# Attention of layer 0 on one core: values weighted by unscaled exponentials, bias and maximum in one VectorE operation, modulation vectors on VectorE

## The chip, the cores and the metric

One Trainium2 chip, of which the program uses one core: TensorE (PE; its loads of the stationary operand are shown as PEld), VectorE (DVE), ScalarE (ACT), GpSimd (POOL) and SyncE (SP), which issues nearly all DMAs here. The metric is the time of one execution on the device, in microseconds; lower is better. Everything is computed in float32, for the large products as sums of three products of halves ("hi" and "lo") of the operands.

## The reference

The whole reference is a block with two layers (layer 0 with a pool mixer and neighbourhood attention, layer 1 with a scan over time) and a second block behind it. The change touches layer 0's attention and the vectors that modulate its later stages. Cut to that:

```python
def context_attention(q, k, v):                       # 256 context tokens, 8 heads of 64
    s = jnp.einsum('bqhd,bkhd->bhqk', q, k) * (NA_HEAD_DIM ** -0.5)
    p = jax.nn.softmax(s, axis=-1)
    return jnp.einsum('bhqk,bkhd->bqhd', p, v).reshape(B, L, D_NA)

def neighbourhood_attention(q, k, v, k_ctx, v_ctx, rpb):   # 512 tokens, a grid of 8 rows by 64
    def row_block(args):
        ...
        s_lat = jnp.where(col_ok[:, None, :], s_lat + bias, NEG_INF)
        s = jnp.concatenate([s_lat.reshape(...), s_ctx], axis=-1)
        p = jax.nn.softmax(s, axis=-1)
        ...
        return (jnp.einsum('bhqrk,brkhd->bqhd', p_lat, v_band)
                + jnp.einsum('bhqc,bchd->bqhd', p_ctx, v_ctx))

mod = silu_c @ ada_w[i] + ada_b[i]                    # six modulation vectors of 1024, twice (x and ctx)
sh1, sc1, gt1, sh2, sc2, gt2 = jnp.split(mod, N_MOD, axis=-1)
```

## The kernel before, in words

The order of instructions on each engine is set by a scheduler that plays the program through with its own estimate of times; the code only gives the data dependences, the buffers and, with `issue_after`, some positions. Each engine then works through its list in order, and a waiting instruction holds up all behind it.

`even_mixer` is the first half of layer 0. After the products for keys, values and queries it calls `attend` six times: twice for the 256 context tokens (`qt` 0 and 1, 128 queries each, 256 keys per head) and four times for the 512 grid tokens (`b` 0 to 3, 128 queries each, 256 keys of a window and the 256 of the context). In each call the heads go in pairs (`hb` 0 to 3). For one head:

- the scores `S` (PSUM tile `a`, 128 queries by 256 or 512 keys) are one or two products on TensorE (lines 1202, 1208, 1210);
- VectorE adds the bias `nab` to the window's half (line 1211) and takes the negated maximum of each row (1212, or 1203 for the context);
- ScalarE takes the exponential with that maximum as bias and the row's sum as a by-product (1214);
- VectorE takes the reciprocal of the sum (1215) and multiplies the exponentials by it (1216);
- `pv` turns the 128 by 128 pieces of the result on TensorE (1241, into PSUM tile `b`), copies them out as `pT` (1243, any engine) and multiplies them with the values. There the values are the stationary operand (128 by 64) and `pT` is the moving one (128 columns), and the two heads of a pair write to two halves of the partitions of the PSUM tile `O` (1247). `O` comes out with channels on partitions, as the next stage wants it.

Behind each pair, `next(self.fill)` places a piece of the pool mixer's products (18 products, lines 590 to 592) and now and then its VectorE and ScalarE work (`pool_group`, lines 1161 to 1179). `pump` places one step of `ada_vec`: a group of 256 columns of the modulation weights is loaded in four pieces (`adaw`, two buffers) and multiplied with the two input vectors in 16 steps (`ada_step`), either by ScalarE and GpSimd together (lines 729, 732 and 733: scale on one, add on the other) or, where `on_dve` is true, by VectorE alone (725 and 727). Twelve such groups belong to this stage: six run before `attend` on VectorE, and from line 1142 on, where `on_dve` is set to false, six on ScalarE and GpSimd. `ada_sum` turns the sums on TensorE (745) and adds them up (747, 751).

When the six calls are over, the last piece of the pool mixer has to be finished (VectorE's chain of lines 1169 to 1176, TensorE's line 1178) before the next stage's products (`evout`, lines 590 to 592 again) find their inputs; these are split into halves by lines 596 and 597, and their weights by 583 and 584.

Of the kernel before, what the change touches and what calls it, by code (L numbers as in the profile page):

```python
# [10 lines left out]
F32 = mybir.dt.float32  # L11
# [3 lines left out]
AF = mybir.ActivationFunctionType  # L15
ALU = mybir.AluOpType
AX = mybir.AxisListType
# [532 lines left out]
class Prog:  # L550
# [496 lines left out]
    def even_mixer(self, act, ap, kv, h):  # L1047

        tc, nc = self.tc, self.nc
# [7 lines left out]
        def cols(ps, w, m, g):  # L1057
            _, v, n, o = g
            for k in range(8):
                s = slice(k * 256 + m * 128, k * 256 + (m + 1) * 128)  # L1060
                bi = self.mm3(ps[:, :n], (w[0][:, s], w[1][:, s]), h(k, g), k == 0, k == 7)
            return bi
# [3 lines left out]
        for u, g in self.pair_order(4, self.halves(groups)):  # L1066
            _, v, n, o = g
# [12 lines left out]
        with ExitStack() as ctx:  # L1080
            E = ctx.enter_context
            p1 = E(tc.tile_pool(name="ev1", bufs=2))
            p2 = E(tc.tile_pool(name="ev2", bufs=2))
# [6 lines left out]
            for u in (6, 7):  # L1090
                w = self.wsplit(self.i["evin"][u])
                c0 = (u - 6) * 256
                for tt in range(6):
                    ps = self.pt("mm")
                    for k in range(8):
                        s = slice(k * 256, (k + 1) * 256)
                        hk = h(k, ("x" if tt < 4 else "c", 0, 128, tt * 128))
                        bi = self.mm3(ps[:, :256], hk, (w[0][:, s], w[1][:, s]), k == 0, k == 7)
                    if tt % 3 == 2:
                        self.pump(bi)  # L1100
                    if tt < 4:
                        vs = p1.tile([128, 256], F32, name="vs", tag="psum_w")
# [5 lines left out]
            for u in (2, 3):  # L1108
                w = self.wsplit(self.i["evin"][u])
                for m in range(2):  # L1110
                    mb = u * 2 + m - 4
                    for g in groups:
                        n = g[2]
                        ps = self.pt("mm")
                        bi = cols(ps, w, m, g)
# [9 lines left out]
            def pooling():  # L1125
                for u in (0, 1):
                    w = self.wsplit(self.i["evin"][u])
                    for m in range(2):
                        pss = [self.pt("mm") for g in groups]
                        for k in range(8):  # L1130
                            s = slice(k * 256 + m * 128, k * 256 + (m + 1) * 128)
                            for ps, g in zip(pss, groups):
                                self.mm3(ps[:, :g[2]], (w[0][:, s], w[1][:, s]), h(k, g), k == 0, k == 7)
                            yield
                        for ps, g in zip(pss, groups):
                            self.pool_group(p1, u * 2 + m, ps, g[2], g[3], poolw, po)
# [2 lines left out]
            self.adatag = "st"  # L1139

            self.fill = pooling()
            self.on_dve = False
            for qt in range(2):
                self.attend(p2, qt, None, qP, kT, vd, vctx, *ahl)
            for b in range(4):
# [33 lines left out]
        nc.scalar.activation(po[:, gi, o:o + n], ps[:, :n], AF.Copy, scale=self.col("psc", gi))  # L1179

    def attend(self, p2, qt, b, qP, kT, vd, vctx, chi, clo):
        nc = self.nc
        O = self.pt("st")
        if b is not None:
            ws = WSTART[b]
            vwin = p2.tile([128, 2, 512], F32, name="vwin", tag="vwin")
            for r in range(8):
                nc.sync.dma_start(vwin[(r % 4) * 32:(r % 4) * 32 + 32, r // 4, :], vd[r * 64 + ws:r * 64 + ws + 32, :])
        for hb in range(4):
            if b is not None:  # L1190
                nab = p2.tile([128, 2, 256], F32, name="nab", tag="nab")
                nc.sync.dma_start(nab, self.i["nab"][b][:, hb * 512:(hb + 1) * 512].rearrange("p (h k) -> p h k", h=2))
            es = []
            for hh in range(2):
                r = slice(hh * 64, hh * 64 + 64)
                S = self.pt("a")
                e = p2.tile([128, 512], F32, name="e", tag="e", bufs=3)
                m = p2.tile([128, 4], F32, name="m", tag="m", bufs=4)
                if b is None:
                    n = 256  # L1200
                    q = qP[r, hb, NX + qt * 128:NX + (qt + 1) * 128]
                    nc.tensor.matmul(S[:, :256], q, kT[r, hb, NX:], start=True, stop=True)
                    nc.vector.tensor_reduce(m[:, 0:1], S[:, :256], AX.X, ALU.max, negate=True)
                    vs = [vctx[:, 0], vctx[:, 1]]
                else:
                    n = 512
                    q = qP[r, hb, b * 128:(b + 1) * 128]
                    nc.tensor.matmul(S[:, :256], q, kT[r, hb, :NX].rearrange("p (r c) -> p r c", c=64)[:, :, ws:ws + 32],
                                     start=True, stop=True)
                    nc.tensor.matmul(S[:, 256:], q, kT[r, hb, NX:], start=True, stop=True)  # L1210
                    nc.vector.tensor_tensor(S[:, :256], S[:, :256], nab[:, hh, :], ALU.add)
                    nc.vector.tensor_reduce(m[:, 0:1], S, AX.X, ALU.max, negate=True)
                    vs = [vwin[:, 0], vwin[:, 1], vctx[:, 0], vctx[:, 1]]
                nc.scalar.activation(e[:, :n], S[:, :n], AF.Exp, bias=m[:, 0:1], accum_out=m[:, 1:2])
                nc.vector.reciprocal(m[:, 2:3], m[:, 1:2])
                nc.vector.tensor_scalar(e[:, :n], e[:, :n], m[:, 2:3], None, ALU.mult)
                es.append(e[:, :n])
            bi = self.pv(p2, O[:, hb * 128:(hb + 1) * 128], es, [[v[:, h * 64:(h + 1) * 64] for v in vs] for h in (hb * 2, hb * 2 + 1)])
            for _ in range(1 if b is None else 1 + hb % 2):
                with self.tc.issue_after(bi.ins):  # L1220
                    next(self.fill, None)
            if hb == 3 and (b is not None or qt == 0):
                self.pump(bi)
        if b is None:
            o = NX + qt * 128
            dst = lambda t: t[:, :, o:o + 128]
            src = O.rearrange("p (k t) -> p k t", k=4)
        else:
            dst = lambda t: t[:, :, :NX].rearrange("p k (r b c) -> p k r b c", r=8, b=4)[:, :, :, b, :]
            src = O.rearrange("p (k r c) -> p k r c", k=4, r=8)  # L1230
        self.split_sb(dst(chi), dst(clo), src)
# [677 lines left out]
    def causal(self, t2, i, kind, mask, Q, K, vm, QD, KD, vdt, chi, clo):  # L1909
        nc = self.nc  # L1910
        n = (i + 1) * 128
        qs = slice(i * 128, (i + 1) * 128)
        O = self.pt("st")
        v = vm if kind == 0 else vdt
        for hb in range(4):
            es = []
            for h in (hb * 2, hb * 2 + 1):
# [13 lines left out]
                es.append(s[:, :n])  # L1931
            self.pv(t2, O[:, hb * 128:(hb + 1) * 128], es, [[v[:, k, h * 64:(h + 1) * 64] for k in range(i + 1)] for h in (hb * 2, hb * 2 + 1)])
        kb = slice(kind * 4, kind * 4 + 4)
        self.split_sb(chi[:, kb, qs], clo[:, kb, qs], O.rearrange("p (k t) -> p k t", k=4))

# [17 lines left out]
```

## Time and profile before

| | before |
|---|---|
| median of 3 runs | 3166.5 us (3166.19 to 3166.78) |
| profiled execution, its own time | 3169.68 us |
| span of its profile | 3167.8 us |
| granted TensorE clock, mean over the span | 0.923 |
| PE busy | 2825.9 us (89%) |
| PEld busy | 2343.8 us (74%) |
| DVE busy | 1786.6 us (56%) |
| ACT busy | 1552.0 us (49%) |
| POOL busy | 1138.5 us (36%) |

Busy time is an average over very different stages. The stage of the change lies between about 174 us (the first scores) and 345 us (the next stage's products run), some 5% of the span. Records of TensorE are pipelined and their ends are modelled, so in its rows the distance from one start to the next counts, not the length of a record. A float32 product shows as two records (two passes), a turn as one.

### The profile page before, as it was taken

How to read it: one execution, taken by the hardware profiler on the slowest of the kernel's cores; microseconds unless marked ns; L12 is line 12 of the kernel's file. 1: busy time of each engine (PE TensorE's matmuls, PEld its weight loads, DVE VectorE, ACT ScalarE, POOL GpSimd, SP SyncE). 2: the span in 40 equal slices, each digit the busy share in tenths (PEclk: the TensorE clock that was granted, in tenths of full speed). 3: DMA queues.
4: the chain of work that ended last, by engine and by line, in shares of the span. 5: the costliest groups of instructions: out<-in, count | busy, mean ns of one | idle time of the engine just before them, and what ended most of it. 6: DMA issues, size and time to landing. Idle time of an engine off the chain costs nothing.

```text
span 3167.8 us, 50960 instructions
## 1 busy us (share of the span) xinstructions
PE 2825.9 (89%) x19290; PEld 2343.8 (74%) x19290; DVE 1786.6 (56%) x3557; ACT 1552.0 (49%) x3104; POOL 1138.5 (36%) x1500
## 2 busy tenths in 40 slices
PE   6999889999996899886777769699997999989999
PEld 6967778888885688764666658577876885678887
DVE  8466383444448725758688732644456654556364
ACT  3246556666664633554566532455543444544341
POOL 4013436667675212045666640245543110010000
PEclk9989989999998899987688879799998996999999
DMA  5323213333331565432223231244541220022222
GB/s 224 127 82 98 104 50 128 117 126 127 113 114 61 190 194 156 162 123 84 73 96 103 79 113 53 99 171 170 179 150 56 80 87 7 14 80 90 103 96 85
DMA packets 137589, 345.69 MB, mean 109 GB/s; under 512 B 16385, under 2 KB 48769, under 8 KB 120065
## 3 DMA queue, kind: packets, MB, share of 16 engines
q1 hardware_dynamic: 137344, 342.43, 31.6%
q8 instruction: 153, 2.51, 0.3%
q14 instruction: 92, 0.75, 0.1%
HBM read 293.35 MB, written 49.02 MB: 108 GB/s over the span
## 4 chain that ended last, share of the span: by engine, by line
PE 34%; DVE 8%; ACT 6%; POOL 5%; DMA 4%; issue 2%; SPq 0%; ACTq 0%; POOLq 0%; DVEq 0%
PE mm L590 7%; PE mm L591 7%; PE mm L592 7%; POOL acc L733 2%; DMA adaw<-in_ada_dram 2%; PE a L1288 2%; ACT wh L583 1%; PE st L1247 1%; PE a L329 1%; POOL M L428 1%; POOL Mt L427 1%; PE y L520 1%; DVE G L387 1%; PE a L1920 1%; PE a L1923 1%
## 5 line engine op out<-in xcount | busy, mean ns | idle before, releaser
L733 POOL TENSOR_TENSOR acc<-acc,adat 128x256 f32<-128x256 f32 x658 | 574.9, 896 | 539.2 <-ACT acc L729 434.0
L584 DVE TENSOR_TENSOR wl<-wr,wh 128x2048 fp32r<-128x2048 f32 (+3 forms) x145 | 317.6, 2190 | 361.1 <-ACT wh L583 358.7
L732 ACT ACTIVATE adat<-adaw,silu 128x256 f32<-128x256 f32 x644 | 319.4, 508 | 262.9 <-POOL acc L733 164.0
L583 ACT CAST wh<-wr 128x2048 fp32r<-128x2048 f32 (+2 forms) x147 | 266.8, 1815 | 232.1 <-PE mm L591 218.7
L590 PE MATMUL mm<-fh,wh 128*128 128x512 f32 (+1 forms) x1008 | 350.2, 356 | 14.0 <-DVE relu L1015 9.8
L591 PE MATMUL mm<-fl,wh 128*128 128x512 f32 (+1 forms) x1008 | 353.1, 352 | 2.2 <-DVE fl L597 2.2
L592 PE MATMUL mm<-fh,wl 128*128 128x512 f32 (+1 forms) x1008 | 352.0, 351 | 0.9 <-DVE wl L584 0.9
L590 PE MATMUL mm<-h_xhi,wh 128*128 128x512 f32 (+1 forms) x784 | 277.7, 359 | 3.6 <-ACT h_xhi L596 2.5
L591 PE MATMUL mm<-h_xlo,wh 128*128 128x512 f32 (+1 forms) x784 | 278.2, 357 | 1.8 <-DVE h_xlo L686 1.5
L592 PE MATMUL mm<-h_xhi,wl 128*128 128x512 f32 (+1 forms) x784 | 278.1, 357 | 0.0
L664 POOL TENSOR_TENSOR acc<-acc,t 128x256 f32<-128x256 f32 x127 | 109.1, 867 | 345.0 <-ACT t L662 342.2
L590 PEld LDWEIGHTS mm<-fh,wh 128*128 128x128 f32 x1008 | 192.1, 191 | 42.1 <-DVE relu L1015 12.1
L591 PEld LDWEIGHTS mm<-fl,wh 128*128 128x128 f32 x1008 | 191.7, 190 | 27.6 <-DVE fl L597 4.0
L592 PEld LDWEIGHTS mm<-fh,wl 128*128 128x128 f32 x1008 | 192.0, 191 | 26.2 <-DVE wl L584 1.1
L1039 DVE TENSOR_TENSOR y<-mm,y 128x512 f32<-128x512 f32 (+1 forms) x184 | 99.5, 559 | 152.1 <-PE mm L592 151.6
L590 PE MATMUL mm<-h_hi,wh 128*128 128x512 f32 (+1 forms) x408 | 160.7, 398 | 6.3 <-ACT h_hi L685 6.3
L592 PEld LDWEIGHTS mm<-h_xhi,wl 128*128 128x128 f32 x784 | 149.0, 190 | 21.4 <-issue 0.2
L590 PEld LDWEIGHTS mm<-h_xhi,wh 128*128 128x128 f32 x784 | 147.6, 190 | 23.3 <-ACT h_xhi L596 2.8
L591 PEld LDWEIGHTS mm<-h_xlo,wh 128*128 128x128 f32 x784 | 148.9, 191 | 20.8 <-DVE h_xlo L686 1.7
L427 POOL TENSOR_TENSOR Mt<-M 128x30 f32<-128x30 f32 (+14 forms) x240 | 141.7, 591 | 58.1 <-PE f L443 23.6
L591 PE MATMUL mm<-h_lo,wh 128*128 128x512 f32 (+1 forms) x408 | 160.3, 394 | 0.0
L592 PE MATMUL mm<-h_hi,wl 128*128 128x512 f32 (+1 forms) x408 | 159.6, 393 | 0.0
(451 smaller groups left out, 6929.6 us busy)
## 6 DMA issues: line engine op xcount, KB each, us to landing
adaw<-in_ada_dram SPq DMA_DIRECT2D x256, 256.0 KB, 2.7
wr<-in_w_dram SPq DMA_DIRECT2D x64, 1024.0 KB, 4.8
wr<-in_wup_dram SPq DMA_DIRECT2D x22, 1024.0 KB, 4.7
base<-b SPq DMA_DIRECT2D x32, 384.0 KB, 3.1
ZU<-vt SPq DMA_DIRECT2D x192, 64.0 KB, 2.5
wr<-in_wdn_dram SPq DMA_DIRECT2D x16, 704.0 KB, 4.1
wr<-in_win_dram SPq DMA_DIRECT2D x9, 1024.0 KB, 4.7
wr<-in_evin_dram SPq DMA_DIRECT2D x8, 1024.0 KB, 4.8
```

The costliest lines, as they stand in the source:

```text
L329: nc.tensor.matmul(ps[:, c], bk[g][:, c0 + c].rearrange("p a t -> p (a t)"), G[:, :na, c0 + c, :], start=True, stop=True)
L427: nc.gpsimd.tensor_tensor(t, a, b, ALU.mult)
L583: nc.scalar.copy(hi[:, :n], raw[:, :n])
L584: (eng or nc.vector).tensor_tensor(lo[:, :n], raw[:, :n], hi[:, :n], ALU.subtract)
L590: mm(out, lhs[0], rhs[0], start=first, stop=False)
L591: mm(out, lhs[0], rhs[1], start=False, stop=False)
L592: return mm(out, lhs[1], rhs[0], start=False, stop=last)
L664: nc.gpsimd.tensor_tensor(acc, acc, sq, ALU.add)
L732: nc.scalar.activation(t, w, AF.Copy, scale=s)
L733: nc.gpsimd.tensor_tensor(acc, acc, t, ALU.add)
L1039: nc.vector.tensor_tensor(yb, ps[:, :n], yb, ALU.add)
L1288: bi = nc.tensor.matmul(ps[:, :256], wcol(m, k), z[:, k, o], start=k == 0, stop=k == early - 1)
```

## The change

`attend` is rewritten from the scores on:

- for the grid tokens one VectorE operation adds the bias to all 512 scores, negates the sum, writes it to `e` in SBUF and takes the row's minimum; the bias tile `nab` is 512 wide now, its second half filled with zeros by GpSimd. The exponential reads `e` in SBUF with scale -1 in place of `S` in PSUM;
- the exponentials are not scaled. They are turned and copied out (the first head of a pair by VectorE, the second by ScalarE), and in the product with the values `pT` is the stationary operand (128 by 128) and the values are the moving one (64 columns). `O` now has queries on partitions;
- once per call, the reciprocals of eight sums are taken and `O` (128 by 512) is multiplied by them into `o`, and four turns on TensorE bring `o` to the layout that `O` had;
- the line `on_dve = False` ahead of the calls is gone: all twelve groups of modulation columns of this stage are computed by VectorE. (`mlp` sets it to false later, as before.)

```diff
             self.fill = pooling()
-            self.on_dve = False
...
         O = self.pt("st")
+        m = p2.tile([128, 4, 8], F32, name="m", tag="m", bufs=3)
...
-                nab = p2.tile([128, 2, 256], F32, name="nab", tag="nab")
-                nc.sync.dma_start(nab, self.i["nab"][b][:, hb * 512:(hb + 1) * 512].rearrange("p (h k) -> p h k", h=2))
-            es = []
+                nab = p2.tile([128, 2, 512], F32, name="nab", tag="nab")
+                nc.gpsimd.memset(nab[:, :, 256:], 0.0)
+                nc.sync.dma_start(nab[:, :, :256], self.i["nab"][b][:, hb * 512:(hb + 1) * 512].rearrange("p (h k) -> p h k", h=2))
...
-                    nc.vector.tensor_tensor(S[:, :256], S[:, :256], nab[:, hh, :], ALU.add)
-                    nc.vector.tensor_reduce(m[:, 0:1], S, AX.X, ALU.max, negate=True)
...
-                nc.scalar.activation(e[:, :n], S[:, :n], AF.Exp, bias=m[:, 0:1], accum_out=m[:, 1:2])
-                nc.vector.reciprocal(m[:, 2:3], m[:, 1:2])
-                nc.vector.tensor_scalar(e[:, :n], e[:, :n], m[:, 2:3], None, ALU.mult)
-                es.append(e[:, :n])
-            bi = self.pv(p2, O[:, hb * 128:(hb + 1) * 128], es, [[v[:, h * 64:(h + 1) * 64] for v in vs] for h in (hb * 2, hb * 2 + 1)])
+                    nc.vector.tensor_tensor_reduce(e, S, nab[:, hh, :], -1.0, 3e38, ALU.add, ALU.min, m[:, 1, h:h + 1])
+                    nc.scalar.activation(e, e, AF.Exp, bias=m[:, 1, h:h + 1], scale=-1.0, accum_out=m[:, 2, h:h + 1])
+                pt = self.pt("b")
+                k = n // 128
+                for i in range(k):
+                    nc.tensor.transpose(pt[:, i * 128:(i + 1) * 128], e[:, i * 128:(i + 1) * 128], self.cst("ident"))
+                pT = p2.tile([128, 512], F32, name="pT", tag="pT", bufs=3)
+                (nc.scalar.copy if hh else nc.vector.tensor_copy)(pT[:, :n], pt[:, :n])
+                for i in range(k):
+                    bi = nc.tensor.matmul(O[:, h * 64:(h + 1) * 64], pT[:, i * 128:(i + 1) * 128], vs[i][:, h * 64:(h + 1) * 64], start=i == 0, stop=i == k - 1)
...
+        nc.vector.reciprocal(m[:, 3], m[:, 2])
+        o = p2.tile([128, 512], F32, name="o", tag="o")
+        nc.vector.tensor_tensor(o.rearrange("p (h c) -> p h c", c=64), O.rearrange("p (h c) -> p h c", c=64),
+                                m[:, 3].unsqueeze(2).to_broadcast([128, 8, 64]), ALU.mult)
+        O = self.pt("b")
+        for k in range(4):
+            nc.tensor.transpose(O[:, k * 128:(k + 1) * 128], o[:, k * 128:(k + 1) * 128], self.cst("ident"))
```

**Place 1, TensorE at the seam between the first two calls of `attend`.** First the list before: turns of the exponentials (`b<-cst,e`), scores (`a<-kT,qP`), products with the values (`st<-pT,vctx`, which come as 64 by 128), and the sums of a modulation group (`st<-cst,acc`).

```order
L592 MATMUL mm<-h_xhi,wl 128x512
L745 MATMUL st<-cst,acc_1581 128x128 x2
L745 MATMUL st<-cst,acc_1582 128x128 x2
L1241 MATMUL b<-cst,e 128x128 x2
L1202 MATMUL a<-kT,qP 128x256
L1241 MATMUL b<-cst,e 128x128 x2
L1202 MATMUL a<-kT,qP 128x256
L1247 MATMUL st<-pT,vctx 64x128 x4
```

Now the same place of the changed kernel (its turns of the exponentials are line 1220, its products with the values line 1224, the four turns of `o` line 1236):

```order
L592 MATMUL mm<-h_xhi,wl 128x512
L745 MATMUL st<-cst,acc_1581 128x128 x2
L745 MATMUL st<-cst,acc_1582 128x128 x2
L1204 MATMUL a<-kT,qP 128x256 x2
L1236 MATMUL b<-cst,o 128x128 x4
L1220 MATMUL b<-cst,e 128x128 x2
L1204 MATMUL a<-kT,qP 128x256 x2
L1224 MATMUL st<-vctx,pT 128x64 x2
L1220 MATMUL b<-cst,e 128x128 x4
L1224 MATMUL st<-vctx,pT 128x64 x2
```

VectorE's list of the changed kernel at that place, where line 1205 is the maximum of a head's scores, 1222 the copy of turned exponentials and 1232 the scaling of `O`:

```order
L1222 COPY pT<-b 128x256
L1205 TENSOR_REDUCE m<-a 128x1 x2
L1230 RECIPROCAL m<-m 128x8
L1222 COPY pT<-b 128x256
L1205 TENSOR_REDUCE m<-a 128x1 x2
L1232 TENSOR_TENSOR o<-st,m 128x512
```

The turns of `o` are new and stand behind only two score products, and the scaling that they need stands on VectorE behind two maxima of those scores. The products with the values are as many as before and come as 128 by 64.

**Place 2, VectorE behind the last call of `attend`.** Before (`psum_w` and `pool_t` are the pool mixer's last piece, `wl` the next stage's weights, `h_xlo` and `a_lo` its inputs, `ada_t` the sum of a modulation group):

```order
L1169 TENSOR_TENSOR psum_w<-up 128x271
L1169 TENSOR_TENSOR psum_w<-psum_w 128x269
L747 TENSOR_REDUCE ada_t<-st 128x4
L1169 TENSOR_TENSOR psum_w<-psum_w 128x265
L751 TENSOR_TENSOR mod_84<-ada_t,cols 128x4
L584 TENSOR_TENSOR wl<-wr,wh 128x2048
L1169 TENSOR_TENSOR psum_w<-psum_w 128x257
L597 TENSOR_TENSOR h_xlo<-po,h_xhi 128x768 x3
L1173 SCALAR_TENSOR_TENSOR pool_t<-psum_w,up 128x240
```

Now, with the numbers of the two sums left in (acc_3016 and acc_3017 are one group of modulation columns):

```order
L1168 TENSOR_TENSOR psum_w<-psum_w 128x265
L751 TENSOR_TENSOR mod_84<-ada_t,cols 128x4
L584 TENSOR_TENSOR wl<-wr,wh 128x2048
L727 SCALAR_TENSOR_TENSOR acc_3017<-adaw,silu,acc_3017 128x256
L727 SCALAR_TENSOR_TENSOR acc_3016<-adaw,silu,acc_3016 128x256
L597 TENSOR_TENSOR h_xlo<-po,h_xhi 128x768
L1168 TENSOR_TENSOR psum_w<-psum_w 128x257
L597 TENSOR_TENSOR h_xlo<-po,h_xhi 128x768 x2
L597 TENSOR_TENSOR a_lo<-b,a_hi 128x4x8x16
L727 SCALAR_TENSOR_TENSOR acc_3017<-adaw,silu,acc_3017 128x256
L727 SCALAR_TENSOR_TENSOR acc_3016<-adaw,silu,acc_3016 128x256
L1172 SCALAR_TENSOR_TENSOR pool_t<-psum_w,up 128x240
```

Between the first `psum_w` of that piece and the end of its first `pool_t` nine modulation steps (725 and 727) now stand on VectorE; before there were none.

**Place 3, TensorE in layer 1, a thousand microseconds later,** whose code the change does not touch but whose order the scheduler drew anew (`mm<-wl,mixh` are layer 1's feature products, `a<-prod,cols` and `a<-G,bk` products of its scan). Before:

```order
L590 MATMUL mm<-wh,mixh 128x256
L591 MATMUL mm<-wl,mixh 128x256
L592 MATMUL mm<-wh,mixl 128x256
L398 MATMUL a<-prod,cols 64x512
L329 MATMUL a<-G,bk 128x128 x4
L329 MATMUL a<-G,bk 128x256 x2
L590 MATMUL mm<-wh,mixh 128x256
L591 MATMUL mm<-wl,mixh 128x256
```

Now:

```order
L592 MATMUL mm<-wh,mixl 128x256
L590 MATMUL mm<-wh,mixh 128x256
L398 MATMUL a<-prod,cols 64x512
L329 MATMUL a<-G,bk 128x128 x4
L329 MATMUL a<-G,bk 128x256 x2
L591 MATMUL mm<-wl,mixh 128x256
```

The three groups of the scan moved behind some twenty feature products; from here to the end of the scan there are many such moves on all engines, and no instruction more or less.

## Rows read from the trace of the kernel before

**Rows 1.** Busy time by stretch; columns: PE, PEld, DVE, ACT, POOL, clock, DMA, GB/s

```profile
200.00:321.40 121.40, 120.67 (x781) 85.36 (x781) 80.86 (x205) 82.52 (x199) 41.96 (x68) 1.00 0.27 83
321.40:332.00 10.60, 0.64 (x6) 0.39 (x4) 10.42 (x16) 6.49 (x10) 6.00 (x6) 0.68 0.35 127
```

**Rows 2.** Waits of PE, 200 to 320 us, all of them: total, times, longest

```profile
PE st L1178 <- DVE pool_t L1176: 0.4, 1, 0.4
PE st L1247 <- ACT pT L1243: 0.3, 1, 0.3
```

**Rows 3.** Timeline of PE, one pair of heads: start, length, operation, count

```profile
252.76 0.66 PE L1241 MATMUL b<-cst,e 128*128 128x128 f32 x4
253.35 0.43 PE L1247 MATMUL st<-pT,vwin 128*64 128x128 f32 x2
253.72 0.70 PE L1208 MATMUL a<-kT,qP 64*128 64x256 f32 x2
...
255.36 0.54 PE L1247 MATMUL st<-pT,vwin 128*64 128x128 f32 x5
...
256.38 0.39 PE L590 MATMUL mm<-h_chi,wh 128*128 128x256 f32 x1
```

**Rows 4.** Timeline of PE, a context pair's last six passes and the product behind

```profile
197.44 0.65 PE L1247 MATMUL st<-pT,vctx 128*64 128x128 f32 x6
198.02 0.39 PE L590 MATMUL mm<-h_chi,wh 128*128 128x256 f32 x1
```

**Rows 5.** PE: line L1241 (shortest/median/longest, ns); timeline, eight passes, 128 and 2 moving

```profile
L1241 PE MATMUL b<-cst,e x150: 270/273/332, 196.1 to 317.3; 128*128 128x128 f32 x150
...
233.16 1.03 PE L1241 MATMUL b<-cst,e 128*128 128x128 f32 x8
...
1136.57 0.95 PE L1483 MATMUL st<-cst,sq 128*128 128x2 f32 x8
```

**Rows 6.** DVE by line, attention (L1926: second block): busy us, mean ns, idle

```profile
L1212 DVE TENSOR_REDUCE m<-a 128x1 f32<-128x512 f32 x32 | 21.9, 687 | 0.6
L1216 DVE TENSOR_SCALAR e<-e,m 128x512 f32<-128x512 f32 x32 | 16.4, 514 | 0.7
L1211 DVE TENSOR_TENSOR a<-a,nab 128x256 f32<-128x256 f32 x32 | 13.8, 430 | 16.2 <-PE a L1210 16.2
...
L1926 DVE CUSTOM_DVE_ANT_0 s<-a,c_mcaus 128x512 f32<-128x512 f32 x8 | 5.5, 692 | 3.4 <-PE b L1241 3.2 <-PE a L1920 0.2
...
L1243 DVE COPY pT<-b 128x512 f32<-128x512 f32 x2 | 1.4, 684 | 1.0 <-PE b L1241 1.0
...
L727 DVE SCALAR_TENSOR_TENSOR acc<-adaw,silu,acc 128x256 f32<-128x256 f32 x14 | 6.4, 477 | 0.0
```

**Rows 7.** Timeline of the first pair of heads, ACT and PE

```profile
178.35 0.47 ACT L1214 ACTIVATE e<-a,m 128x256 f32<-128x256 f32 x1
...
180.58 0.69 PE L1241 MATMUL b<-cst,e 128*128 128x128 f32 x2
```

**Rows 8.** Timeline behind the last call (DVE, PE, ACT)

```profile
325.89 3.75 DVE L597 TENSOR_TENSOR h_xlo<-po,h_xhi 128x768 fp32r<-128x768 f32 x3
329.55 0.92 DVE L1173 SCALAR_TENSOR_TENSOR pool_t<-psum_w,up 128x240 f32<-128x240 f32 x1
...
332.00 1.19 PE L1178 MATMUL st<-pool_t,poolw 128*128 128x256 f32 x2 [9.96 <-DVE pool_t L1176]
...
342.66 0.90 ACT L729 ACTIVATE acc<-adaw,silu 128x256 f32<-128x256 f32 x2
...
344.33 0.97 PE L590 MATMUL mm<-h_xhi,wh 128*128 128x256 f32 x4 [2.53 <-ACT h_xhi L596]
```

**Rows 9.** DVE by line, 173 to 325 us, then 7 to 50 us beside POOL

```profile
L1173 DVE SCALAR_TENSOR_TENSOR pool_t<-psum_w,up 128x240 f32<-128x240 f32 x3 | 1.2, 403 | 0.0
...
L727 DVE SCALAR_TENSOR_TENSOR acc<-h_chi,silu,acc 128x256 f32<-128x256 f32 x14 | 11.3, 870 | 0.0
```

**Rows 10.** Chain that ended last, 1430 to 1440 us: a product group in the scan

```profile
1433.94 1.94 PE a L398 x2
```

More of the change, by code (lines that the diff above doesn't have):

```diff
@@ L1190, in attend @@
             if b is not None:
-                nab = p2.tile([128, 2, 256], F32, name="nab", tag="nab")
-                nc.sync.dma_start(nab, self.i["nab"][b][:, hb * 512:(hb + 1) * 512].rearrange("p (h k) -> p h k", h=2))
-            es = []
+                nab = p2.tile([128, 2, 512], F32, name="nab", tag="nab")
+                nc.gpsimd.memset(nab[:, :, 256:], 0.0)
+                nc.sync.dma_start(nab[:, :, :256], self.i["nab"][b][:, hb * 512:(hb + 1) * 512].rearrange("p (h k) -> p h k", h=2))
             for hh in range(2):
+                h = hb * 2 + hh
                 r = slice(hh * 64, hh * 64 + 64)
@@ L1197, in attend @@
                 e = p2.tile([128, 512], F32, name="e", tag="e", bufs=3)
-                m = p2.tile([128, 4], F32, name="m", tag="m", bufs=4)
                 if b is None:
@@ L1202, in attend @@
                     nc.tensor.matmul(S[:, :256], q, kT[r, hb, NX:], start=True, stop=True)
-                    nc.vector.tensor_reduce(m[:, 0:1], S[:, :256], AX.X, ALU.max, negate=True)
+                    nc.vector.tensor_reduce(m[:, 1, h:h + 1], S[:, :256], AX.X, ALU.max, negate=True)
                     vs = [vctx[:, 0], vctx[:, 1]]
+                    nc.scalar.activation(e[:, :n], S[:, :n], AF.Exp, bias=m[:, 1, h:h + 1], accum_out=m[:, 2, h:h + 1])
                 else:
```

## The prediction, as put on record

> **What bounds the kernel now.** I read the busy time by stretch first [rows 1]. [...] Since the ends of PE's records are modelled, a busy PE need not be a full one; so I read PE's waits next [rows 2]: from 200 to 320 us they come to 0.7 us in two pieces. PE works through its list without a gap, and all softmax work on DVE and ACT lies beside the mixer's products. In this stretch the time is what TensorE's list costs; taking operations from DVE there gives nothing, adding passes to PE costs in full. The third reading is the tail. From 321.4 to 332 us PE has 0.64 us of work [rows 1] and waits 9.96 us in one piece for DVE's `pool_t`, then 2.53 us for ACT's `h_xhi` [rows 8]; there DVE's list is the time, busy 10.42 of 10.60 us [rows 1]. At the start, while no mixer products fill the gaps, the first pair of heads shows the bare chain: the first exponential starts at 178.35 us and takes 0.47, the turns start at 180.58 [rows 7]. So the prediction has four places: PE's list, the start, stalls that DVE may now cause, and DVE's list in the tail.
>
> **PE's list.** Scores, turns of exponentials and mixer products stay as many. What changes is the product with the values: as many passes, but with 128 stationary columns and 64 moving ones in place of 64 and 128. Before, a pair of window heads has 16 passes, in two runs from start to next start: 253.35 to 253.72 and 255.36 to 256.38, 0.37 + 1.02 = 1.39 us [rows 3]. A pair of context heads has 8: 0.37 for the first two as there, 197.44 to 198.02 = 0.58 for six, 0.95 together [rows 3, 4]. For the new form the trace has two neighbours. A turn has 128 stationary and 128 moving columns: one has a record of 0.27 us, eight in a row take 1.03 [rows 5], so the step from one to the next is (1.03 - 0.27) / 7 = 0.109. Four turns with the change to the next kind take 252.76 to 253.35 = 0.59 us [rows 3]. The other neighbour, L1483, has 128 stationary and only 2 moving columns, and eight of them still take 0.95 us [rows 5], (0.95 - 0.27) / 7 = 0.10 each if a lone one has the same record. So with 128 stationary columns a pass costs about the same whether 128 or 2 columns move, and 64 lies between: I take 0.109, the upper, since the 0.59 us of a run is read from turns; the lower is 0.10, and 0.009 on 320 passes is 2.9 us.
>
> [...]
>
> A window head now has one run of eight passes, 0.59 + 4 x 0.109 = 1.03 us, a pair 2.06: 0.67 more than 1.39, times 16 pairs **+10.7 us**. A context head has a run of four, 0.59, a pair 1.18: 0.23 more, times 8 pairs **+1.8**. The four turns of `o` are new, 0.59 in each of six calls: **+3.5**. Together **+16.0** (bounds 13 and 18, the upper if the finer cutting into runs adds 0.04 at each of some 50 runs).
>
> **The start.** The chain of the first pair loses the reciprocal and the multiplication between exponential and turns. Of the 1.76 us from 178.82 to 180.58 [rows 7] part is the second head's and part semaphores; I take **-2** for the first pairs, before mixer work covers it (0 if the scores come no earlier, -5 if all four pairs gain).
>
> **Stalls by DVE.** Per pair of window heads DVE loses 2 x (0.430 + 0.687 + 0.514) = 3.26 us. It gains two combined operations, for which the nearest row is L1926, a custom operation on 128x512 of 0.692, and one copy of 0.684: 2.07 [rows 6]. That is 1.2 less, times 16 = 19 us. Six scalings of `O`, 128x512 out of PSUM as the maximum's 0.687, give back 4. Four modulation groups of 16 steps fall into the calls, 64 x 0.477 = 30.5 us [rows 6]. DVE's work in the stretch goes from 80.86 by 30.5 + 4 - 19 to about 96, in a stretch grown to 137 us: 70%. On average it fits; but the steps come in bursts of 16 x 0.477 = 7.6 us, and each step waits for its piece of weights ahead of all that is queued behind it, a wait that was ACT's before. What stands behind a step on DVE is a maximum, a copy `pT` or the scaling of `O`; PE waits for all three, and its list has few mixer products at the seams. At the first seam the turns of `o` stand behind two score products only, while the scaling they need stands behind two maxima of these scores: about 0.7 + 0.35 for maxima and scaling and half a microsecond of hand-overs, 1.6 us. In the last call copies stand behind modulation steps, about three of them, 1.5. I take **+3**. The bounds are 0 (each seam covered as the 0.7 us of waits are now) and +10.
>
> ACT and POOL lose the 96 steps. Nothing in the stretch waits for either, so this is worth nothing there.
>
> **The tail.** Nine modulation steps now stand between the first `psum_w` and `pool_t`: 9 x 0.477 = +4.3 us. Against it, POOL no longer has its adds then: beside POOL a step took 0.870 [rows 9] where 0.477 is its mean here [rows 6], and in this tail `pool_t` (L1173, 240 columns) 0.92 [rows 8] in place of 0.403 [rows 9]; that one gives 0.5. The three `h_xlo` took 3.75 us, 1.25 each; shortened in a milder ratio, by 0.39 each, they give 1.2, and the smaller ones about 1: -2.7. Finally ACT's two scalings of a modulation step, 0.90 us, stood ahead of the `h_xhi` for which PE waited 2.53 [rows 8]: -0.9. Sum **+0.7** (bounds -2, if all of the tail's operations shrink as the step did, and +4.5 with no relief).
>
> [...]
>
> **Layer 1.** Its code is the same, but its order is drawn anew: groups of about 1.94 us [rows 10] move behind other work and some in front. I take **0**, with 6 us, three such groups, either way.
>
> **Sum.** 16.0 - 2 + 3 + 0.7 + 0 = +17.7. The profiled execution took 3169.68, so 3187.4; the median is 3.2 us under that execution, hence **3184 us**, +0.56%. About 0.2%, 6.3 us, is what a measurement of this kernel can tell from no change.
>
> **The rivals.**
> A: the passes go by their moving columns. Then 64 columns cost half a turn's step, 0.055, and a run has the fixed part 0.59 - 4 x 0.109 = 0.15: a window pair takes 2 x 0.59 = 1.19 in place of 1.39, -3.2 in all, a context pair 0.75 in place of 0.95, -1.6. With +3.5, -2, +3 and +0.7 that is +0.4: **3167 us**, no change, and faster if the start gives its 5 us and the stalls stay out. For it: PE is a pipeline that can load ahead. Against it: L1483, where 2 columns still cost 0.10. It decides from a pass below about 0.075. Chance 0.12.
> [...] Chance 0.04.
> C: DVE becomes the bound in the bursts. If each of the four holds PE for half its 7.6 us, because the copies and maxima behind it are needed at once or the weights come late, it costs 15 + 1.6 in place of 3: +31.3, **3198 us**. For it: PE's order has no slack written in, and DVE's queue is strict. Against it: 30% of DVE is still free. Chance 0.12.
> D: layer 1's order moves the time by more than 6 us: **3175 or 3193 us**, either as likely. Chance 0.17.
>
> **How the numbers follow.** The forecast has 0.55; its own range is 3175 to 3193. Half of A and the lowest of D lie under 3167, half of C and B above 3198: some 0.18 left out, so the range is 3167 to 3198. Faster needs A with its gains or D downwards with the low bounds: 0.06. Within 6.3 us of 3166.5 lie most of A and the low edge of the forecast: 0.14. Slower: 0.80.
>
> **What the profile after would show.** [...] The forecast is wrong if a pass goes under 0.09, or if DVE's bursts hold up more than a few turns.

## The result, and the profile after

| | before | changed kernel |
|---|---|---|
| first comparison, median (runs) | 3166.64 us (4) | 3203.93 us (4; 3193.7 to 3208.84) |
| ratio, 95% interval | | 1.0098 (1.0078 to 1.0118) |
| second comparison | 3175.31 us (23; 3152.82 to 3181.1) | 3198.0 us (6; 3192.39 to 3206.29) |
| ratio, 95% interval | | 1.0074 (1.0055 to 1.0093) |
| span of the first profile | 3167.8 us | 3206.7 us |

The change makes the kernel slower, by the two ratios 23 and 31 us; 18 were forecast. The first median lies 6 us above the forecast's range; its ratio, on 3166.5, gives 3197.5, just inside. The question is where the time went, since the profile puts only a part of it into the stage of the change. I cut both traces at the same products: the stage (first score product to the last product of the mixer), layer 1's scan (first product for its bonus to the last of its state), and the second block's attention, whose code is the same. In the kernel before these take 167.2, 682.4 and 130.9 us. Busy time by stretch (columns as in [rows 1]), the three stretches before:

```profile
173.60:340.80 167.20, 151.78 (x904) 105.92 (x905) 112.77 (x273) 104.84 (x251) 55.99 (x84) 0.91 0.26 85
1291.20:1973.60 682.40, 542.73 (x6805) 431.20 (x6806) 444.44 (x978) 342.30 (x803) 321.11 (x528) 0.83 0.29 94
2610.10:2741.00 130.90, 124.16 (x584) 70.95 (x582) 70.86 (x329) 70.02 (x201) 0.00 (x0) 0.76 0.03 12
```

And in the changed kernel:

```profile
174.60:355.10 180.50, 159.77 (x927) 124.68 (x928) 114.70 (x291) 63.42 (x147) 8.35 (x28) 0.90 0.25 79
1310.80:2008.80 698.00, 552.75 (x6792) 441.94 (x6793) 444.85 (x977) 338.65 (x802) 319.26 (x528) 0.80 0.28 91
2642.60:2780.40 137.80, 132.18 (x581) 75.79 (x582) 70.87 (x329) 70.14 (x201) 0.00 (x0) 0.70 0.03 11
```

The stage is 13.3 us longer, the scan 15.6, the second attention 6.9. To the code of the last two nothing was added (the scan's stretch even has fifteen products fewer, which now stand ahead of it), and in the last even the order of the instructions is that of before; what differs there is the granted clock, 0.70 where before had 0.76.

Inside the stage, the timeline of PE (start, length, operation, count) shows the new products and the tail:

```profile
330.38 0.56 PE L1224 MATMUL st<-vwin,pT 128*128 128x64 f32 x4
330.78 0.61 PE L1224 MATMUL st<-vctx,pT 128*128 128x64 f32 x4
331.22 0.66 PE L1224 MATMUL st<-vwin,pT 128*128 128x64 f32 x4
331.72 0.61 PE L1224 MATMUL st<-vctx,pT 128*128 128x64 f32 x4
332.14 0.36 PE L590 MATMUL mm<-h_chi,wh 128*128 128x256 f32 x1
...
334.76 0.60 PE L1236 MATMUL b<-cst,o 128*128 128x128 f32 x4
346.11 1.19 PE L1177 MATMUL st<-pool_t,poolw 128*128 128x256 f32 x2 [10.75 <-DVE pool_t L1175]
```

Two heads' sixteen passes take 330.38 to 332.14 = 1.76 us, 0.11 a pass; the two runs of [rows 3] took 1.39. The step between single starts is 0.111 or 0.112 us in 216 of 279. The wait for `pool_t` is 10.75 us (9.96 before). PE's waits from 200 us to the end of the calls (total, times, longest), 0.7 us in [rows 2], are now:

```profile
PE st L1224 <- DVE pT L1222: 1.7, 2, 0.9
PE st L1224 <- issue: 1.3, 1, 1.3
PE a L1204 <- ACT e L1207: 1.0, 1, 1.0
PE b L1220 <- DVE pT L1222: 0.8, 1, 0.8
PE st L1224 <- ACT pT L1222: 0.5, 2, 0.2
```

5.3 us. VectorE's groups in the calls (busy, mean ns of one, idle before):

```profile
L727 DVE SCALAR_TENSOR_TENSOR acc<-adaw,silu,acc 128x256 f32<-128x256 f32 x70 | 30.6, 478 | 0.3 <-DMA adaw<-in_ada_dram 0.2
L1215 DVE CUSTOM_DVE_ANT_0 e<-a,nab 128x512 f32<-128x512 f32 x32 | 21.8, 686 | 12.3 <-PE a L1213 6.5 <-issue 3.5 <-ACT po L1178 1.7
L1222 DVE COPY pT<-b 128x512 f32<-128x512 f32 x16 | 11.0, 689 | 12.5 <-PE b L1220 12.2 <-PE st L1224 0.3
L1232 DVE TENSOR_TENSOR o<-st,m 128x512 f32<-128x512 f32 x6 | 4.2, 692 | 8.8 <-PE st L1224 8.7
```

The combined operation, the copy, the scaling and the step cost what the neighbouring rows said (0.686, 0.689, 0.692, 0.478 us), and the step waits for its weights 0.2 us in all. In the tail, VectorE's groups are these:

```profile
L727 DVE SCALAR_TENSOR_TENSOR acc<-adaw,silu,acc 128x256 f32<-128x256 f32 x10 | 4.4, 481 | 0.0
L597 DVE TENSOR_TENSOR h_xlo<-po,h_xhi 128x768 fp32r<-128x768 f32 x3 | 2.8, 954 | 0.0
L1172 DVE SCALAR_TENSOR_TENSOR pool_t<-psum_w,up 128x240 f32<-128x240 f32 x1 | 0.4, 404 | 0.0
```

With POOL quiet (0.00 us of work from 334.76 to 346.11 us) `h_xlo` takes 0.95 us in place of 1.25 and `pool_t` 0.40 in place of 0.92 [rows 8], so that the steps inserted cost 0.8 us of wait. That it is POOL, the kernels of the next section bear out: where the modulation stays on POOL, two of the three `h_xlo` take 1.47 to 1.48 us, and where it is on VectorE all three take 0.94 to 0.95.

### The profile page after: what moved, and what is told of

Same layout as the page of the kernel before. It is cut to its first block, busy times and chain, and to the rows that moved or that the text cites. A ratio compares the mean times of both kernels' runs of the same rounds, so it can differ in the third digit from the quotient of the medians.

```text
span 3206.7 us, 50819 instructions
## 1 busy us (share of the span) xinstructions
PE 2854.5 (89%) x19314; PEld 2380.8 (74%) x19314; DVE 1795.7 (56%) x3591; ACT 1501.8 (47%) x2986; POOL 1079.8 (34%) x1432
## 5 line engine op out<-in xcount | busy, mean ns | idle before, releaser
L733 POOL TENSOR_TENSOR acc<-acc,adat 128x256 f32<-128x256 f32 x574 | 509.1, 910 | 356.8 <-ACT acc L729 255.8
L732 ACT ACTIVATE adat<-adaw,silu 128x256 f32<-128x256 f32 x560 | 278.1, 508 | 251.6 <-POOL acc L733 152.5
L590 PE MATMUL mm<-fh,wh 128*128 128x512 f32 (+1 forms) x1008 | 350.6, 356 | 14.1 <-DVE relu L1015 9.6
```

The lines of the kernel that those rows point to most:

```text
L590: mm(out, lhs[0], rhs[0], start=first, stop=False)
L732: nc.scalar.activation(t, w, AF.Copy, scale=s)
L733: nc.gpsimd.tensor_tensor(acc, acc, t, ALU.add)
```

## The experiments

Of each kernel I compare the three lengths. One thing stands in the way: in the stage TensorE is granted its lower level (0.5 of full speed in the trace's clock records, which hold only this and 1.0) for a while at the start, where it waits 1.8 us for the first queries and 4.7 for the first exponential, and again in the tail, where it waits for `pool_t`. For how long differs, above all at the start: 20.5 + 10.2 = 30.7 us before, 27.3 + 10.2 = 37.5 in the first profile of the changed kernel (all from the trace's clock records). The first run shows what that is worth.

**The changed kernel again.** No edit.

> The changed kernel once more. Stage of the change = from the first score product to the mixer's last product (167.2 us before, 180.6 in the first profile of the changed kernel); scan = from layer 1's first bonus product to the last product of its state (680.7 to 696.3 there, +15.6); second block's attention 130.9 to 137.8. Theory (the order drawn anew makes layer 1 longer): stage 180 to 181 and scan within 4 us of 696. Rival (chance of the clock's two levels): the scan and the second attention fall anywhere between 681 and 697, 131 and 138, with a different share at the lower clock.

Its stretches:

```profile
173.80:349.70 175.90, 155.17 (x927) 121.83 (x928) 114.58 (x291) 63.44 (x147) 8.37 (x28) 0.92 0.26 82
1302.90:1990.10 687.20, 536.84 (x6792) 427.54 (x6793) 444.50 (x977) 339.03 (x803) 320.67 (x528) 0.83 0.29 93
```

The stage had 27.3 us of the lower level here and is 175.9 us long; a third execution with the same order of the stage (scan_as_before, below) had 44.4 and took 184.1. Half a microsecond per microsecond of the lower level brings 180.5, 175.9 and 184.1 to 177.1, 177.6 and 177.3 at the 30.7 of before. So **the change costs the stage 10 us** at an equal share of the lower level, and all lengths of it below are also given at 30.7. This is an estimate: counting the lower level only where TensorE works moves no length by more than about a microsecond. The scan is 10.8 us shorter than in the first profile, with the same order and a clock of 0.83 in place of 0.80, so my bounds of 180 to 181 for the stage and of 4 us for the scan did not hold. The first profile is of the slowest of its four runs, this one of the fastest of its six.

**Parts of the change alone.** The products alone (unscaled exponentials, `pT` stationary, scaling and turns of `o` once per call), as a difference to the changed kernel:

```diff
             self.fill = pooling()
+            self.on_dve = False
...
-                    nc.vector.tensor_tensor_reduce(e, S, nab[:, hh, :], -1.0, 3e38, ALU.add, ALU.min, m[:, 1, h:h + 1])
-                    nc.scalar.activation(e, e, AF.Exp, bias=m[:, 1, h:h + 1], scale=-1.0, accum_out=m[:, 2, h:h + 1])
+                    nc.vector.tensor_tensor(S[:, :256], S[:, :256], nab[:, hh, :], ALU.add)
+                    nc.vector.tensor_reduce(m[:, 1, h:h + 1], S, AX.X, ALU.max, negate=True)
+                    nc.scalar.activation(e, S, AF.Exp, bias=m[:, 1, h:h + 1], accum_out=m[:, 2, h:h + 1])
```

> Kernel before with the new products alone: unscaled exponentials, turned exponentials stationary, values moving, scaling and turns of o once per call. Bias, maximum and modulation as before. Theory: products +8, turns of o +3, so the stage is 177 to 181 us. Rival (the stage's growth comes from VectorE's new work): 168 to 171. The scan has an order of its own here: by the theory of the order its length is neither 681 nor 696 for a reason in the stage, and it may be anything from 675 to 700.

The change without its modulation part, by the first line of that difference alone:

> Changed kernel, but the 96 modulation steps stay on ScalarE and GpSimd as before. Its list on TensorE in the scan is that of the changed kernel row by row, while its order in the layers ahead is another. Theory (products with the values and turns of o are the stage's cost, modulation nearly none): stage 176 to 181, and scan 692 to 700 as in the changed kernel, 3190 to 3205 in all. Rival (bursts of modulation steps on VectorE hold PE): stage 170 to 173.

The kernel before with the modulation part alone, by the same line taken out of it:

> Kernel before, with the 96 modulation steps on VectorE and nothing else changed. Theory: in the stretch where PE is the bound nothing, in the tail up to +4.5 less 3.6: stage 166 to 170. Rival (bursts hold PE, more so as VectorE keeps its three separate operations per head here): 175 to 185.

The kernel before with the combined operation alone:

```diff
...
-                    nc.vector.tensor_tensor(S[:, :256], S[:, :256], nab[:, hh, :], ALU.add)
-                    nc.vector.tensor_reduce(m[:, 0:1], S, AX.X, ALU.max, negate=True)
+                    nc.vector.tensor_tensor_reduce(e, S, nab[:, hh, :], -1.0, 3e38, ALU.add, ALU.min, m[:, 0:1])
...
```

(The wider `nab` and the exponential that reads `e` come with it, as in the change.)

> Kernel before with bias and maximum in one operation and nothing else changed. Theory (PE is the bound there, VectorE's relief gives nothing): stage 166 to 168 at the kernel before's 31 us of the lower clock. Rival (a shorter chain per head is worth something): stage 160 to 164.

And both of the latter, the change without its products:

> Changed kernel without the new products: scaled exponentials, values stationary as before, but bias and maximum in one operation and the 96 modulation steps on VectorE. Theory (only the products and turns of o lengthen the stage): stage 166 to 170. Rival (VectorE's modulation with fewer operations around it still holds PE): 173 to 178. The scan has an order of its own; in all 0.995 to 1.003.

| kernel | stage as traced | lower level | at 30.7 us of it | to before | whole time, ratio (interval) |
|---|---|---|---|---|---|
| before | 167.2 | 30.7 | 167.2 | | |
| products | 176.6 | 37.5 | 173.2 | +6.0 | 1.0028 (1.0016 to 1.004) |
| modulation | 170.2 | 34.1 | 168.5 | +1.3 | 0.9986 (0.9969 to 1.0004) |
| combined operation | 154.6 | 20.5 | 159.7 | -7.5 | 0.9975 (0.9958 to 0.9992) |
| combined, modulation | 162.1 | 34.1 | 160.4 | -6.8 | 0.9924 (0.9907 to 0.9941) |
| products, combined | 177.4 | 37.5 | 174.0 | +6.8 | 1.0076 (1.0058 to 1.0094) |
| all three | 180.5, 175.9, 184.1 | 37.5, 27.3, 44.4 | 177.3 | +10.1 | 1.0098, 1.0074 |

Modulation did what was expected: it is worth 1.3 us alone, and 3.3 on top of the other two, about the 2.2 that the forecast holds for it (1.5 of the stalls, 0.7 of the tail); nothing like C. The products alone came out at 173.2, under the 177 to 181 expected and above the rival's 168 to 171, yet on top of the other two parts they cost 16.9. And the combined operation alone shortens the stage by 7.5 us, though it only takes work from VectorE, for which TensorE waited 0.7 us in the calls. My theory that such relief gives nothing fell there; the kernel without the products, too, lies under the 166 to 170 expected, and its ratio under the 0.995 to 1.003. TensorE's own timeline shows where the time went. One head's window scores in the kernel before:

```profile
259.62 0.70 PE L1208 MATMUL a<-kT,qP 64*128 64x256 f32 x2
260.16 0.59 PE L1210 MATMUL a<-kT,qP 64*128 64x256 f32 x2
260.68 0.39 PE L590 MATMUL mm<-h_chi,wh 128*128 128x256 f32 x1
```

Two heads' scores, neighbours in the list, with the combined operation:

```profile
252.27 0.71 PE L1209 MATMUL a<-kT,qP 64*128 64x256 f32 x4
252.80 0.60 PE L1211 MATMUL a<-kT,qP 64*128 64x256 f32 x4
253.34 0.43 PE L1250 MATMUL st<-pT,vwin 128*64 128x128 f32 x2
```

Four passes take 259.62 to 260.68 = 1.06 us, and eight 252.27 to 253.34 = 1.07: the two heads lie on the two halves of the rows and run at once, if nothing stands between them. In the timeline of the kernel with the combined operation 10 of 16 pairs stand side by side, where before had 2 (not 3, as the expectations below have it). Its window scores take 23.8 us in place of 32.3, start to start: 8.5 less, about what the stage gained. A shorter wait for VectorE's chain is not the reason, since TensorE's waits in the calls grew from 0.7 to 2.4 us:

```profile
PE st L1250 <- ACT pT L1246: 1.4, 3, 0.8
PE st L1250 <- DVE ada_t L747: 1.0, 1, 1.0
```

Why the scheduler puts them side by side is not shown. The combined operation leaves its sum in SBUF, so that the score tile is free after one operation on VectorE and not only after the exponential; but the products alone, without that, have 7 such pairs, and the changed kernel, with it, only 5. So the combined operation, worth 7.5 us alone, is worth nothing on top of the products (+6.0 and +6.8).

**Scores placed in pairs.** To test these neighbours as a cause, the scores of a pair are issued behind the previous pair's last turn, when both tiles are free:

```diff
-                    nc.tensor.matmul(S[:, 256:], q, kT[r, hb, NX:], start=True, stop=True)
...
+                    with self.tc.issue_after(self.lastT):
...
+                        nc.tensor.matmul(S[:, 256:], q, kT[r, hb, NX:], start=True, stop=True)
...
-                nc.tensor.transpose(pt[:, i * 128:(i + 1) * 128], e[:, i * 128:(i + 1) * 128], self.cst("ident"))
+                self.lastT = nc.tensor.transpose(pt[:, i * 128:(i + 1) * 128], e[:, i * 128:(i + 1) * 128], self.cst("ident")).ins
```

In the kernel before, in the changed kernel, and in the one without the products:

> Kernel before, same instructions, but the score products of a pair of window heads are placed behind the previous pair's last turn, so that both heads' scores stand next to each other in 16 of 16 pairs (3 of 16 before). Theory (two heads' scores, one on each half of the rows, run at once when they are neighbours: 1.06 us for one head's four passes, 1.07 for two heads' eight): 13 x 1.05 = 13.7 us less, given back by up to 6 us of new waits for the softmax, so a stage of 154 to 160 against 167. Rival (the shorter stages of the kernels with bias and maximum in one operation come from VectorE's shorter chain, not from the order of the scores): 166 to 172.

> Changed kernel with the same placement of the scores (15 or 16 pairs together in place of 5). Theory: 10 to 11 x 1.05 less, so a stage of 166 to 172 at some 31 us of the lower clock (178 for the changed kernel at that share); what is left over the kernel above with the same placement is the products and the turns of o, 9 to 12 us. Rival: 176 to 182.

> The kernel without the new products (one operation for bias and maximum, modulation on VectorE), with the scores placed in pairs (15 of 16 in place of 9). Theory: 6 us less than its 162, 154 to 159, and as good a time as any so far, 0.990 to 0.996 of before, the scan's order being its own. Rival (VectorE's chain behind two heads at once becomes the wait): 160 to 166.

TensorE's time in score passes (start to start, waits behind them included) falls from 47.6 to 35.7 us in the kernel before and from 44.8 to 33.3 in the changed one, but only from 41.2 to 39.9 in the third. Eight passes again take 1.07. Only the changed kernel's stage came as expected: 173.9 as traced and 170.5 at 30.7 us (-6.8). That of before is 176.7 and 168.2 (+1.0), that without the products 175.8 and 163.8 (+3.4): at 30.7 both lie in their rivals' ranges, so two expectations of three missed, and with them the 0.990 to 0.996 of the last. The lower level lasted 37.5, 47.8 and 54.6 us; in the last two, 17.1 and 20.4 us of it fall into the middle of the calls, where the same two kernels without pairs have none. If the new waits brought it, which is not shown, it belongs to the price of the pairs, and by the traced lengths these two stages are 9.5 and 13.7 us longer, not 1.0 and 3.4. PE's waits in the calls of the kernel before with pairs:

```profile
PE b L1242 <- DVE e L1217: 9.1, 14, 1.5
PE b L1242 <- DVE pool_t L1176: 3.7, 3, 2.3
PE st L1248 <- DVE pT L1244: 2.5, 2, 1.7
PE b L1242 <- DVE m L1216: 2.1, 2, 1.7
```

And of the changed kernel with pairs:

```profile
PE st L1227 <- DVE pT L1225: 4.2, 4, 1.3
PE b L1221 <- ACT e L1217: 2.4, 4, 0.7
PE b L1221 <- DVE pT L1225: 1.3, 1, 1.3
```

In the first of these kernels L1217 is VectorE's scaling of the exponentials (in the second, ScalarE's exponential itself). With both heads' scores coming at once, TensorE waits for the scaling 14 times; where the exponentials go unscaled, that wait is not there. So it is shown that neighbouring scores run at once and that this shortens TensorE's list; the stage kept the saving in one kernel of three, and in the other two the waits for the chain behind the scores took it back. In all, these three ran at 1.005 (1.0035 to 1.0065), 1.0059 (1.0036 to 1.0082) and 1.0013 (1.0001 to 1.0025): the last is 0.9 per cent more than without pairs, and the rest of the differences lies outside the stage.

**The order far from the edit.** Stage and total do not go together in these kernels. To part them, one tile and one memset were added at the start of layer 1:

```diff
+            dum = self.small.tile([128, 256], F32, name="dum", tag="dum")
+            nc.vector.memset(dum, 0.0)
```

In the changed kernel:

> Changed kernel with one tile of 256 columns and one memset on VectorE (well under 1 us) added at the start of layer 1. That alone turns the order of layer 1's scan, on all five engines, back into that of the kernel before, while all up to it stays that of the changed kernel. Theory (the order of the scan carries the part of the loss that the stage does not): scan 680 to 687 us, stage still 175 to 181, and over the kernel before only 10 to 15 us are left, ratio 1.003 to 1.005. Rival (the scan's order is worth nothing; chance of the clock, or something else that the new stage leaves behind): the ratio stays at 1.007 to 1.008, scan 687 to 698.

In the kernel before, which was also profiled once more without it:

> Kernel before with the one tile and memset (well under 1 us) of the kernel scan_as_before. No instruction of the work differs from before; up to the scan its order is that of before, in the scan a third order, and behind the scan (the second block's attention) the order that scan_as_before and no_prod have there. Theory (orders that the scheduler draws anew, far from any edit, move the time by as much as the edit does): stage 167 us as before, second attention 117 to 127 against 131 to 134, and the time moves by more than 0.2% of before, most likely down, 0.993 to 0.998. Rival (the second attention's length follows chance, not its order; the order is worth nothing): second attention 130 to 138, ratio 0.999 to 1.001.

> Kernel before once more, for a second profile. Theory of the order: scan within 5 us of 682.4, second block's attention anywhere between 131 and 138. Rival (chance): the scan too is 5 to 15 us away from 682.4.

Stretches of the changed kernel with the tile: stage, scan, second attention.

```profile
175.10:359.20 184.10, 163.48 (x927) 127.36 (x928) 114.67 (x291) 63.33 (x147) 8.38 (x28) 0.88 0.25 78
1310.10:1993.70 683.60, 545.29 (x6809) 432.98 (x6809) 444.59 (x978) 341.67 (x803) 320.98 (x528) 0.83 0.29 94
2632.80:2759.00 126.20, 120.16 (x581) 69.26 (x582) 72.03 (x331) 69.25 (x199) 0.00 (x0) 0.76 0.03 12
```

Of the kernel before with the tile:

```profile
174.80:342.20 167.40, 151.96 (x903) 106.14 (x904) 112.75 (x273) 104.70 (x251) 55.94 (x84) 0.91 0.28 85
1292.50:1989.00 696.50, 551.33 (x6807) 443.95 (x6808) 448.88 (x978) 339.99 (x803) 314.45 (x528) 0.81 0.29 92
2625.00:2741.20 116.20, 109.35 (x582) 63.54 (x582) 71.72 (x331) 68.58 (x198) 0.00 (x0) 0.86 0.04 13
```

Of the kernel before again:

```profile
173.50:340.40 166.90, 151.49 (x903) 105.82 (x904) 112.68 (x273) 104.70 (x251) 55.94 (x84) 0.91 0.27 85
1290.80:1975.50 684.70, 546.70 (x6809) 434.95 (x6810) 444.14 (x978) 341.44 (x803) 321.13 (x528) 0.83 0.29 94
2609.90:2743.50 133.60, 127.08 (x584) 72.42 (x582) 70.82 (x329) 70.05 (x201) 0.00 (x0) 0.74 0.03 11
```

The changed kernel with the tile ran at 1.0019 (1.0002 to 1.0036) of before in place of 1.0074, less than the 1.003 to 1.005 expected: far from the edit, the order that the scheduler draws moves the whole time by half a per cent. Where in the kernel that lies rests on single profiles. With the scan's order of before the scan takes 682.4, 684.7 and 683.6 us, the last with the changed kernel's stage; with that of the changed kernel 698.0, 687.2 and 692.8 (the one with its modulation back on ScalarE has that order too): 9 us apart in the mean. But two kernels with pairs, whose order there is nearly that of before (28 of VectorE's 978 instructions moved), take 690.9 and 689.8. And the clock goes with it: the lower level lasted 225, 236 and 232 us in the first three, 276, 236 and 270 in the next. Where both had 236 us of it, the scan took 684.7 and 687.2. So an order that costs 9 us by itself is not shown; what differs is mostly the time at the lower level, and whether the order brings that on is open.

The tile also changes the order in the second attention, which I had not said; there it takes 126.2 us, and 116.2 and 117.6 in the two other kernels with the same order there (the kernel before with the tile, the one without the products), against 126.5 to 138 in the nine profiles with the order of before there. The shortest of the nine is the changed kernel with pairs:

```profile
2629.20:2755.70 126.50, 119.72 (x582) 68.89 (x582) 70.86 (x329) 69.83 (x201) 0.00 (x0) 0.79 0.03 12
```

Here too the clock carries the difference: the lower level lasts 33 to 60 us in the three and 53 to 83 in the nine, and the length less half of that time is 96 to 100 us in every profile, whatever the order. The kernel before with the tile, by my estimate half a microsecond of work (VectorE's operations on 128 by 256 take 0.35 to 0.48 us in the stage), ran at 1.0025 (1.0012 to 1.0037): up, where I expected down. In its one profile, of the fastest of its twelve runs, a longer scan (+14.1) and a shorter second attention (-14.7) cancel, so that profile does not show where the rise comes from.

This bears on the fastest kernel too. Without the products (0.9924, 24 us less than before) the stage gives 7 us of it; its second attention is 13 to 16 us shorter, in an order that the edit did not ask for, with 39 us at the lower level in place of 64 and 70.

## Why the prediction was half right

- **What bounds the kernel.** TensorE's list does bound the stage; but "taking operations from DVE there gives nothing" failed. The list's length depends on which passes are neighbours; what made them so here is not shown.
- **PE's list.** The step was right (0.109 forecast, 0.111 to 0.112 measured); A (0.055) and B (0.162) fell. No run shows the 0.053 that B adds to a pass for its load; what the runs show is the 0.111 to 0.112 from one pass to the next, loads included, and in the trace of before the load of the last of the eight turns in [rows 5] starts at 233.82 us, with the product ahead of its own, which follows at 233.93: loads do go ahead, as A says. The lower bound of 0.10 was a misreading: the starts of the passes with 2 moving columns are 0.111 to 0.112 apart too, but for the first two of a run. The run was mis-sized: 0.91 us in the median for a window head in place of 1.03, 0.48 in place of 0.59 for a context head and 0.49 for the turns of `o`, since a run of these passes costs hardly anything beside its steps (eight of 0.111 are 0.89). Value products: from 30.4 to 38.4 us (36.8 in the second profile), +6 to +8 in place of +12.5; turns of `o` 2.8 in place of 3.5. The scores, counted at nothing, gave back 2.8 (4.5 in the second profile).
- **The start.** The first turns come 5.4 us behind the first scores in place of 7.0, -1.6 for -2; the lower clock then lasted from 3 us less to 14 longer in three executions of one and the same stage, which no term held.
- **Stalls.** +3 forecast; PE's waits grew by 4.6 us, none at the turns of `o` of the first seam, where 1.6 were forecast, and most at the copies `pT`.
- **The tail.** +0.8 at `pool_t`, -1.3 at `h_xhi` and +0.6 at `h_xlo`, in sum 0.1, by the mechanism forecast: +0.7 was near.
- **The stage in all.** 16 - 2 + 3 + 0.7 = 17.7 was forecast, 10 measured at equal clock: right in kind, too large by the runs and the scores.
- **Layer 1.** "I take 0, with 6 us" is the step that failed: what lies outside the stage cost 13 to 21 us, and with the tile's other order half a per cent of the whole time came back. D had this with 0.17, at a price too small. In the scan it is 9 us in the mean of three profiles each, most of it with more time at the lower level; in the 160 us ahead of it 3 to 4 (157.2 before, 161.4 and 159.9 after, 159.0 with the order of before), of which the fifteen products that moved there are some 2. So the stage was forecast 7 us too high, and what lies outside it 13 to 21 too low. The two errors have opposite signs, and that the sum came so near is in part luck.
- **What is left open.** Whether the order of the scan and of the second attention decides how long TensorE stays at the lower level there, or chance does. Over whole executions the mean granted clock was 0.915 in the changed kernel's ten runs and 0.922 in the twelve with the tile, against 0.920 and 0.921 before, which speaks for the order; single profiles of one program differ by 10.8 us in the scan, which speaks for chance beside it. The second attention's 137.8 and 136.8 against 130.9 and 133.6 with one and the same order may be chance: the five more profiles with that order lie between 126.5 and 138.

## What to carry to other kernels

Before costing an operation off the bound engine at nothing, look at what becomes of the bound engine's list: here an edit on VectorE changed which products are neighbours on TensorE, and two that run at once are worth 1.05 us a pair. In these rows, with 128 stationary columns, narrowing the moving operand from 128 to 64 columns saved nothing (0.109 us a pass with 128, 0.111 to 0.112 with 64); two heads' scores on 64 rows each took 1.07 us side by side, where one alone took 1.06; and two value passes with 64 stationary columns each took 0.109 together, as much as one turn with 128. And where a scheduler draws the whole program's order, compare the stage and the total apart, put the time at the lower clock beside every length, and add an edit without work as a control: here it moved the total by 0.25 and by half a per cent.

## What the runs showed of the hardware

- Two heads' score passes on separate halves of the rows: eight in 1.07 us, four of one head in 1.06.
- A pass with 128 stationary columns has a step of 0.11 us: 0.109 with 128 moving columns, 0.111 to 0.112 with 64 and with 2. The value products before, whose two heads wrote to two halves of the columns, were started in twos, 7 and 102 ns apart: two for the price of one.
- The same instructions in the same order took 175.9 to 184.1 us in the stage, by how long TensorE stayed at the lower level (a granted clock of 0.5) around and behind a wait of 4.7 us: half a microsecond for each.
- The second attention took 116 to 138 us in fourteen profiles; less half of its 33 to 83 us at that level it is 96 to 100 in all of them.
- Beside POOL's adds two of three VectorE operations on 128 by 768 took 1.47 to 1.48 us; with POOL quiet each took 0.94 to 0.95.
